# A rebuilt opening: input first, sums of squares partly on TensorE, eight input products open, weights' low parts on GpSimd

## The chip, the cores and the metric

One core of a Trainium2 chip. The time is the device time of one execution in microseconds. The engines are TensorE (PE, its weight loads PEld), VectorE (DVE), ScalarE (ACT), GpSimd (POOL) and SyncE (SP), which here issues all DMAs.

## The reference

A trunk of two layers, on x of 512 tokens by 1024 channels in float32. Each layer is a token mixer followed by a gated convolutional FFN (2816 hidden channels); both sit between norms:

```
h = rmsnorm(x, g0) * (1 + scale) + shift     # adaLN: shift, scale, gate from silu(c) @ ada_w + ada_b
x = x + gate * rmsnorm(mixer(h), g1)
```

The mixer of layer 0 is the RG-LRU: `gate_br, x_br = split(h @ w_in)`, a causal convolution of width 4 over x_br, two sigmoid gates by block-diagonal products, a first-order recurrence over the tokens, `(gelu(gate_br) * hs) @ w_out`. That of layer 1 is gated linear attention. The change is in the kernel's first sublayer, RG-LRU with the norm before it, and in helpers that all sublayers use.

## The kernel before

**Layout.** Channels lie on the 128 partitions and tokens on the free axis: x is eight tiles (KD = 8) of 128 channels by 512 tokens, in one constant buffer. A product accumulates over eight input tiles in one PSUM bank of 512 columns.

**Products in parts.** For precision each float32 operand is split into a high part (rounded to the format that PE multiplies fast, `FR`) and a low part (the rest). `mm3` issues three matmuls: high by high, high by low, low by high. For weights, `load_upto` loads a unit of up to 1024 columns into a `raw` buffer; ACT rounds it into the first half of a `w` buffer (`acopy`) and DVE subtracts to get the second half (`tt`). There are 8 `w`, 3 `raw` and 2 `araw` buffers; `mm` has 7 PSUM banks, `nr` the eighth.

**Order of the work.** Every instruction is first recorded by a wrapper of `Emit` with an engine, an estimated duration, what it reads and writes. `Sched.order` then runs a list schedule over these: SP and PE take what is ready in the order of recording, the other engines what has the longest path to the end, and a buffer is taken when its first instruction is placed. The result is a fixed order on each engine; the hardware then follows it with semaphores. So the durations in `mms`, `tt` and the others time nothing on the chip, but they do set the order.

**The opening.** In the order of recording:

1. Loads: c, x tiles 0 and 1, `par` (all column parameters, 582 columns), the identity, x tiles 2 to 7.
2. The first norm: ACT squares each tile, DVE adds the squares into one tile (`sumsq_add`), PE multiplies that by a column of ones, which gives the sums per token (`rstd_bcast`), ACT scales them, POOL takes the power -0.5 (`pow`), DVE multiplies the identity by each of four columns (a diagonal `dg`), PE multiplies a matrix of ones by that, so that the factor of each token stands on all partitions in PSUM (`rb0`).
3. c is spread over the partitions by PE (`crow`), ACT applies silu (`cact`).
4. For each input tile k: a tile `xn = x * rb0` on DVE; two adaLN columns, each of them a load of 512 KB and one DVE instruction that multiplies and sums (`ada`), finished on ACT (`ada_col`); weight unit `rgx` k; then scale and shift on ACT, rounding on ACT, the low part on DVE; then the products of this tile for NX = 6 output tiles, which stay open in six banks over all k. Tile 0 goes in two halves of 256 tokens (FH = 1).
5. Constants of the decay: some 25 instructions of 8 columns on DVE.
6. `conv4` on each of the six products: one ACT instruction and three on DVE read the bank. The other two outputs (`rgx2`) are then made one after the other, each over all k.
7. The gates: `RGG` says which gate-branch products (`gproj`, one bank, eight input tiles) come ahead of which block's gates. Blocks 0 and 3 multiply raw float32 weights, blocks 1 and 2 in parts (GFR). `recur` does the recurrence of two blocks, `gmul` the last product; `out_proj` follows, by halves of the tokens.

`rstd_from` (steps "power, diagonal, ones") serves every norm in the kernel; in the later ones it works on two columns (256 tokens) at a time, in GLA on four.

adaLN columns of the later sublayers are recorded behind the recurrence (24) and along the FFN (`ada_some`), and fill DVE where their loads have landed.

Of the kernel before, what the change touches and what calls it, by code (L numbers as in the profile page):

```python
# [15 lines left out]
P = 128  # L16
# [8 lines left out]
RGG = ((), (0,), (1,2,3,4), (5,6,7))  # L25
NX = 6
# [4 lines left out]
def unit_list():  # L31
    """Weight units in the order of their use: (key, array name, [(k, m), ...])."""
# [42 lines left out]
# column-parameter layout  # L75
PCOLS = {}
_n = 0
for _name, _w in (("norm_g", 64), ("ffn_conv_w", 2 * 3 * 44), ("ffn_conv_b", 2 * 44),
                  ("rg_conv_w", 32), ("rg_conv_b", 8), ("rg_ba", 8), ("rg_bx", 8),
                  ("rg_lambda", 8), ("gla_b_alpha", 4), ("gla_norm_g", 2), ("ada_b", 96)):  # L80
    PCOLS[_name] = (_n, _w)
    _n += _w
NPAR = _n


class Buf:
    """A tile whose place on the chip is taken when its first instruction is emitted."""
# [10 lines left out]
class View:  # L98
# [12 lines left out]
    def __getitem__(self, sl):  # L111
        """Columns of a plain view."""
        lo = sl.start or 0
        return self.buf[self.lo + lo:self.lo + (self.n if sl.stop is None else sl.stop)]
# [22 lines left out]
ENGS = ("pe", "dve", "act", "pool", "sp")  # L137


class Sched:  # L140
    """Records the kernel's instructions with their operands, orders them by a list schedule
    (deadlines from the longest path to the end, the tensor engine in program order), and
    emits them to Tile in that order."""
# [34 lines left out]
    def order(self):  # L178
# [23 lines left out]
        # allocation order per class  # L202
# [29 lines left out]
        cand = {e: [] for e in ENGS}     # (prio, idx) ready or soon ready  # L232
        wait = {e: [] for e in ENGS}     # (ready, idx)
# [11 lines left out]
        while done < n:  # L245
# [8 lines left out]
            for e in ENGS:  # L254
# [7 lines left out]
                if e == "act" and cand[e]:  # L262
                    # a change of the function table costs time: prefer the present one
                    cand[e].sort(key=lambda c: ops[c[1]].prio +
                                 (TABLE_BIAS if ops[c[1]].table not in (None, table) else 0.0))
                    for j, c in enumerate(cand[e]):
                        if can_alloc(ops[c[1]]):
                            pick = ops[c[1]]
                            del cand[e][j]
                            break  # L270
                    heapq.heapify(cand[e])
                    if pick is None:
                        continue
# [10 lines left out]
                o = pick  # L284
                for b in o.bufs:
                    if not b.live:
                        b.live = True
                        if b.cls in free:
                            free[b.cls] -= 1
                o.start = t  # L290
                dur = o.dur
                if e == "pe":
                    # the clock is halved until the engine has been busy for a while
                    if t - efree[e] > 2.5:
                        warm_at = t + 3.4
                    if t < warm_at:
                        dur *= 2
# [46 lines left out]
class Emit:  # L344
    """Instruction wrappers: costs and operands for the schedule, closures for the emission."""
# [72 lines left out]
    def mms(self, group, after=()):  # L418
        """One schedule item of consecutive matmuls: (out, lhsT, rhs, start, stop[, skip])."""
        dur = 0.0  # L420
        reads, writes = [], []
        for g in group:
            n = g[2].n
            if g[1].buf.dt == FR:
                dur += max(n, 256) * 0.4167e-3 + 0.0025
            else:
                dur += max(n, 118 if n > 1 else 100) * 1.667e-3 + 0.005
            reads += [g[1], g[2]]
            writes.append(g[0])
# [22 lines left out]
KSPLIT = 2                                  # input tiles that come one by one at a sublayer's start  # L452
NAH = 7                                     # products open at a sublayer's start
GWU = ((1, 2, 3), (0,), (0, 1))             # weights in general tiles: two FFNs' pairs, GLA's heads
FH = 1                                      # input tiles taken in halves at the start
TPE = 5                                     # output tiles whose last sum the tensor engine does
GFR = (1, 2)                                # gate blocks multiplied in parts
ADA_A, ADA_B, ADA_F = 24, 4, 4              # adaLN columns per stretch
ADAW = {2: (2, 5), 4: (0, 3, 6), 3: (1, 4, 7)}   # adaLN rows that pass through a weight slot
# [4 lines left out]
def trunk(ctx, tc, xT, wall, adaT, par_d, c_d, walpha_d, ident_d, masks_d, outT):  # L464
# [15 lines left out]
    def gtn(n):  # L480
        """A scratch view of n columns."""
        return (s.buf("gh", F32, 256) if n <= 256 else s.buf("g"))[0:n]
# [12 lines left out]
    x = [xbuf[k * S:(k + 1) * S] for k in range(KD)]  # L495
    e.load(crow[0:D].rows(1), c_d, 4096)

    for k in range(KD):
        e.load(x[k], xT[:, k, :], P * S * 4)
        if k == 1:  # L500
            e.load(par[:], par_d, P * NPAR * 4)
            e.load(ident[:], ident_d, P * P * 4)
    e.memset(ones[:], 1.0)
# [18 lines left out]
    def load_upto(i):  # L522
        while nxt[0] <= min(i, len(UNITS) - 1):
# [9 lines left out]
            if UNITS[j][0] in ingen:  # L533
                # in general tiles, which are plenty at the start of a sublayer
# [8 lines left out]
            if UNITS[j][0][0] == "gz":  # L543
                # 16 columns of either part side by side: one product serves both
# [9 lines left out]
            e.tt(w[D:D + n], raw[0:n], w[0:n].f32(), ALU.subtract)  # L554
# [34 lines left out]
    def rstd_from(nr, nt, dim, act=False):  # L589
        """nr[:, :nt]: sums per token tile -> rstd broadcast to all partitions (PSUM)."""  # L590
# [6 lines left out]
        dg = s.buf("gh", F32, 256) if nt <= 2 else gt()  # L597
        for t in range(nt):
            e.ts(dg[t * P:(t + 1) * P], ident[:], rp[t:t + 1], None, ALU.mult)
        e.mms([(nr[0:nt * P], ones[:], dg[0:nt * P], True, True)])  # L600
# [8 lines left out]
    acc0 = gt()  # L609
    for k in range(KD):  # L610
        sumsq_add(acc0[:], x[k], k == 0)
    rb0 = rstd_bcast(acc0, S, D, True)

# [1 line left out]
    cact = const(D)  # L615
    for i in range(2):
        pc = mmtile()
        e.mms([(pc[:], ones[0:P].rows(1), crow[i * S:(i + 1) * S].rows(1), True, True)])
        e.act(cact[i * S:(i + 1) * S], pc[:], AF.Silu, table="silu")

# [8 lines left out]
    def mod_cols(layer, part, k0=0, k1=KD):  # L629
        """Finish a part: 0/3 shift, 1/4 (1+scale)*norm_g, 2/5 gate*norm_g."""  # L630
# [32 lines left out]
    def h_tile(h, k, sl, rb, n, layer, part_sh):  # L663
        """h = (x * s2) * rstd + shift, in two parts."""
# [7 lines left out]
    def out_proj(src, wkey, klist, gate, nexth, yacc=None):  # L672
        """Last product of a sublayer, y = src @ W (+ yacc); x += gate * rmsnorm(y) * g; then the
        next sublayer's h, or the output. The token halves follow each other, so that the norms
        of one run beside the products of the other."""
# [4 lines left out]
        for sl in HALVES:  # L680
            acc = s.buf("gh", F32, 256)
            ys = []
            for m in range(KD):
# [9 lines left out]
                else:  # L693
                    e.tt(yv, yv, ps[0:n], ALU.add)
                    if end:
                        # the last square by itself, straight into the sum over partitions
# [15 lines left out]
            if nexth is None and sl is HALVES[1]:  # L712
                # the tensor engine, idle by now, takes part of the sums
# [35 lines left out]
    def proj_halves(keys, h_):  # L749
        """First products of a sublayer, by token halves and input tiles as these become ready."""  # L750
# [79 lines left out]
    def ada_col(part, k):  # L830
        """One column of the first norm's shift or scale."""
# [9 lines left out]
    e.stt(b1g[:], pcol("ada_b", 8, KD), 1.0, pcol("norm_g", 0, KD), ALU.add, ALU.mult)  # L841
    h = new_h()
    xps = [mmtile() for _ in range(NX)]
    for k in range(KD):
        # the normalized tile first: shift and scale come from memory later; the first tiles
        # in halves, which go faster through the engines
        parts = HALVES if k < FH else (ALL,)
        xn, hf = gt(), gt()
        hh, hl = h[k]
        for sl in parts:  # L850
            e.tt(xn[sl], x[k][sl], rb0[sl], ALU.mult)
# [3 lines left out]
        for sl in parts:  # L855
            e.act(hf[sl], xn[sl], AF.Identity, bias=mcol(0, 0, k), scale=mcol(0, 1, k))
            e.acopy(hh[sl], hf[sl])
            e.tt(hl[sl], hf[sl], hh[sl].f32(), ALU.subtract)
            for m in range(NX):
                # one reset per bank, before its first half  # L860
# [5 lines left out]
    # decay constants: softplus(-lam) = max(-lam, 0) + log1p(exp(-|lam|))  # L866
# [62 lines left out]
    def recur(ms):  # L929
# [8 lines left out]
        for m in ms:  # L938
            # th = tanh(z), a = exp(-2z): 1 - a = th (1 + a), sqrt(1 - a^2) = sqrt(th) (1 + a)
# [39 lines left out]
    def qk_evac(key, ps):  # L979
        if key[0] == "gz":  # L980
            # rows of z by the two parts of its weights; as an operand: hi, lo, hi
# [82 lines left out]
    def bcol(v, c, j):  # L1064
        """Column j of every block of c, repeated over the block."""
        return v.map(lambda a: a.rearrange("p (n c) -> p n c", c=c)[:, :, j:j + 1].to_broadcast([P, v.n // c, c]))

    def masked(atd, lv, ps, c, lo):
        """Copies the columns lo to c of every block of c where the mask of the level is set."""
# [118 lines left out]
def _unit_sources(i):  # L1188
# [3 lines left out]
    # block-diagonal gates: row tile (block, half), column tiles [wa0 wa1 wx0 wx1]  # L1192
# [58 lines left out]
```

## Time and profile before

| | us |
|---|---|
| median of 3 runs | 1185.19 (1184.75 to 1185.59) |
| span of the profiled execution, first to last instruction | 1182.5 |
| time outside that span, median less span | 2.7 |
| PE, DVE, ACT, POOL busy | 1158.9, 867.3, 553.6, 24.4 |
| first input product, dense run of them | 22.8, 23.8 |
| power -0.5 of the first norm on POOL | starts at 15.55, takes 1.56 |

The profiled execution's own time is its span with what lies around it. A share of busy time is an average over stages: the 98% of PE leaves out that PE is nearly idle in the first 24 us, and the 73% of DVE that DVE is nearly full in the first 185 us. A busy PE is also not a PE at its peak: its pace is read from the number of matmuls in a stretch.

### The profile page before, as it was taken

How to read it: one execution, taken by the hardware profiler on the slowest of the kernel's cores; microseconds unless marked ns; L12 is line 12 of the kernel's file. 1: busy time of each engine (PE TensorE's matmuls, PEld its weight loads, DVE VectorE, ACT ScalarE, POOL GpSimd, SP SyncE). 2: the span in 40 equal slices, each digit the busy share in tenths (PEclk: the TensorE clock that was granted, in tenths of full speed). 3: DMA queues.
4: the chain of work that ended last, by engine and by line, in shares of the span. 5: the costliest groups of instructions: out<-in, count | busy, mean ns of one | idle time of the engine just before them, and what ended most of it. 6: DMA issues, size and time to landing. Idle time of an engine off the chain costs nothing.

```text
span 1182.5 us, 16970 instructions
## 1 busy us (share of the span) xinstructions
PE 1158.9 (98%) x6664; PEld 1017.0 (86%) x6664; DVE 867.3 (73%) x1470; ACT 553.6 (47%) x874; POOL 24.4 (2%) x37
## 2 busy tenths in 40 slices
PE   4999999999999999999999999999999999999998
PEld 3878899988888888899999899999988888888897
DVE  7999999988988956558779767458845556645635
ACT  5688864743333324434478344254643333424421
POOL 1000001000000000000000000000000000000000
PEclk9999999999999999999999999999999999999999
DMA  8956562477787843232412211203243333332202
GB/s 338 312 170 202 200 214 73 160 249 252 249 260 223 261 126 93 88 90 59 144 55 90 72 54 55 72 27 118 72 125 97 100 91 105 90 107 90 72 1 72
DMA packets 45857, 157.44 MB, mean 133 GB/s; under 512 B 4977, under 2 KB 7281, under 8 KB 45778
## 3 DMA queue, kind: packets, MB, share of 16 engines
q1 hardware_dynamic: 45778, 156.36, 41.6%
q8 instruction: 52, 0.85, 0.3%
q14 instruction: 27, 0.22, 0.1%
HBM read 154.25 MB, written 2.10 MB: 132 GB/s over the span
## 4 chain that ended last, share of the span: by engine, by line
PE 90%; DVE 5%; ACT 3%; issue 1%; DMA 1%; SPq 0%; POOL 0%; DVEq 0%; POOLq 0%
PE mm L435 88%; ACT g L411 2%; PE nr L435 1%; DVE g L377 1%; DVE w L364 1%; ACT L411 1%; DVE g L364 1%; ACT w L416 1%; DVE gh L377 1%; DVE g L393 1%; DVE w L377 1%; DMA const<-in_xT_dram 0%; DMA raw<-in_wall_dram 0%; DVE araw L377 0%; SPq L441 0%
## 5 line engine op out<-in xcount | busy, mean ns | idle before, releaser
L435 PE MATMUL mm<-g,w 128*128 128x512 f32 (+1 forms) x5114 | 957.5, 348 | 5.6 <-ACT g L416 2.5
L435 PEld LDWEIGHTS mm<-g,w 128*128 128x128 f32 x5114 | 826.2, 189 | 130.4 <-ACT g L416 4.1
L364 DVE TENSOR_TENSOR w<-raw,w 128x1024 fp32r<-128x1024 f32 (+1 forms) x181 | 217.8, 1205 | 152.4 <-ACT w L416 152.0
L416 ACT CAST w<-raw 128x1024 fp32r<-128x1024 f32 (+1 forms) x181 | 187.2, 1036 | 206.3 <-PE mm L435 202.3
L377 DVE SCALAR_TENSOR_TENSOR g<-mm,const,g 128x511 f32<-128x511 f32 (+3 forms) x208 | 153.3, 745 | 11.2 <-ACT g L411 5.3
L364 DVE TENSOR_TENSOR g<-g,g 128x512 f32<-128x512 f32 (+4 forms) x213 | 126.2, 614 | 37.7 <-ACT g L411 19.4
L411 ACT ACTIVATE g<-mm,const 128x512 f32<-128x512 f32 (+1 forms) x148 | 102.2, 698 | 20.6 <-PE mm L435 20.5
L411 ACT ACTIVATE g<-g 128x512 f32<-128x512 f32 (+1 forms) x132 | 66.7, 540 | 96.2 <-DVE g L377 77.4
L435 PE MATMUL mm<-g,g 128*128 128x256 f32 (+4 forms) x748 | 102.1, 293 | 0.0
L435 PEld LDWEIGHTS mm<-g,g 128*128 128x128 f32 (+1 forms) x748 | 94.8, 191 | 3.8
L416 ACT CAST g<-g 128x512 fp32r<-128x512 f32 (+1 forms) x74 | 45.4, 614 | 107.7 <-DVE g L364 105.0
L377 DVE SCALAR_TENSOR_TENSOR araw<-araw,const 128x1024 f32<-128x1024 f32 x72 | 87.1, 1220 | 9.2 <-DMA araw<-in_adaT_dram 9.0
L364 DVE TENSOR_TENSOR g<-g,mm 128x512 f32<-128x512 f32 (+1 forms) x80 | 44.9, 577 | 44.5 <-PE mm L435 44.2
L364 DVE TENSOR_TENSOR gh<-gh,gh 128x256 f32<-128x256 f32 x97 | 40.4, 420 | 22.2 <-ACT gh L411 20.6
L435 PE MATMUL mm<-w,g 128*128 128x256 f32 x384 | 49.6, 288 | 0.0
L435 PEld LDWEIGHTS mm<-w,g 128*128 128x128 f32 x384 | 46.9, 192 | 1.4 <-issue 1.4
L368 POOL TENSOR_TENSOR sm<-sm,const 128x2 f32<-128x2 f32 (+1 forms) x19 | 19.4, 1022 | 1025.7 <-DVE sm L388 1018.5
L411 ACT ACTIVATE gh<-g 128x256 f32<-128x256 f32 x32 | 13.1, 416 | 51.3 <-DVE g L364 51.3
L411 ACT ACTIVATE g<-gh,const 128x256 fp32r<-128x256 f32 x48 | 21.9, 503 | 26.4 <-DVE gh L377 26.2
L411 ACT ACT_TABLE_LOAD x24 | 30.8, 1283 | 1.1 <-PEq L1242 0.7
L377 DVE SCALAR_TENSOR_TENSOR w<-w,const 128x1024 f32<-128x1024 f32 x24 | 28.8, 1217 | 0.0
L411 ACT ACTIVATE gh<-const 128x256 f32<-128x256 f32 x48 | 18.9, 414 | 20.1 <-DVE const L364 20.0
(66 smaller groups left out, 465.6 us busy)
## 6 DMA issues: line engine op xcount, KB each, us to landing
raw<-in_wall_dram SPq DMA_DIRECT2D x186, 512.0 KB, 3.7
araw<-in_adaT_dram SPq DMA_DIRECT2D x72, 512.0 KB, 4.5
w<-in_adaT_dram SPq DMA_DIRECT2D x24, 512.0 KB, 5.8
raw<-in_wall_dram SPq DMA_DIRECT2D x8, 384.0 KB, 6.7
const<-in_xT_dram SPq DMA_DIRECT2D x8, 256.0 KB, 4.1
out_dram<-const SPq DMA_DIRECT2D x8, 256.0 KB, 2.1
araw<-in_masks_dram SPq DMA_DIRECT2D x1, 512.0 KB, 5.2
const<-in_par_dram SPq DMA_DIRECT2D x1, 291.0 KB, 3.6
```

The costliest lines, as they stand in the source:

```text
L364: self.s.add(eng, dur, lambda: e.tensor_tensor(out.ap(), a.ap(), b.ap(), op=op), [a, b], [out])
L368: lambda: self.nc.gpsimd.tensor_tensor(out.ap(), a.ap(), b.ap(), op=ALU.pow), [a, b], [out])
L377: return self.nc.vector.scalar_tensor_tensor(out.ap(), a.ap(), f(sc), b.ap(), op0=op0, op1=op1, **kw)
L393: lambda: self.nc.vector.tensor_tensor_scan(out.ap(), a.ap(), b.ap(), 0.0, op0=ALU.mult, op1=ALU.add),
L411: return self.nc.scalar.activation(out.ap(), a.ap(), func, **kw)
L416: self.s.add("act", (0.095 if self._sb(a) else 0.052) + out.n * 0.8325e-3, lambda: self.nc.scalar.copy(out.ap(), a.ap()), [a], [out])
L435: r.append(self.nc.tensor.matmul(g[0].ap(), g[1].ap(), g[2].ap(), start=g[3], stop=g[4], **kw))
```

## The change

- **Loads.** c, then all eight tiles of x, then the identity. `par` is laid out anew, with norm weights and adaLN biases first, and loaded in two pieces: 160 columns behind weight unit 0, the rest (422 columns) at input tile 4. Weight unit 0 is loaded ahead of the first adaLN columns.
- **First norm.** The squares are summed in four groups (`SQ_GROUPS`): tiles 0, 1 and 7 alone, tiles 2 to 6 added by DVE as before. PE sums each group into the same four PSUM columns. The table of silu is loaded by an extra instruction at the start.
- **All norms.** No diagonal: PE multiplies the broadcast column (as the stationary operand) by the identity, one matmul per 128 tokens.
- **First tiles.** `h_tile`, as in the other sublayers: one DVE instruction for `x * scale * rstd`, one on ACT (shift and rounding), one on DVE (low part). Tile 0 reads the factor from PSUM, the others from a copy in SBUF made by ACT (`rs0`).
- **Eight products.** NX = 8: all eight outputs are open over all k; the eighth uses the `nr` bank once the factor has been read. The `rgx2` units are gone, `rgx` units have 1024 columns, and RGG is new.
- **Low parts.** The subtraction for `rgx` units 1 to 7 runs on GpSimd.
- **Scheduler.** DVE may be left empty where an instruction that is more urgent by 1.5 us becomes ready before the candidate would end (`LOOK`); durations of matmuls in `mms` are new.

Comments and docstrings are removed too. The core of the diff:

```diff
-RGG = ((), (0,), (1,2,3,4), (5,6,7))
-NX = 6
+RGG = ((0, 1), (2,), (3, 4, 5), (6, 7))
+NX = 8
...
+NPAR0 = 64 + 96
...
+LOOK = ("dve",)
...
                 o = pick
+                if e in LOOK and any(r < t + o.dur - 0.05 and ops[i].prio < o.prio - (r - t) - 1.5 and can_alloc(ops[i])
+                                     for r, i in wait[e]):
+                    heapq.heappush(cand[e], (o.prio, o.idx))
+                    continue
...
             if g[1].buf.dt == FR:
-                dur += max(n, 256) * 0.4167e-3 + 0.0025
+                dur += max(n, 256) * 0.4167e-3 + 0.0135
             else:
-                dur += max(n, 118 if n > 1 else 100) * 1.667e-3 + 0.005
+                dur += 2 * max(n * 0.8333e-3 + 0.002, 0.112)
...
+SQ_GROUPS = ((0,), (1,), (2, 3, 4, 5, 6), (7,))
...
+    e.memset(ones[:], 1.0)
     e.load(crow[0:D].rows(1), c_d, 4096)
     for k in range(KD):
         e.load(x[k], xT[:, k, :], P * S * 4)
-        if k == 1:
-            e.load(par[:], par_d, P * NPAR * 4)
-            e.load(ident[:], ident_d, P * P * 4)
-    e.memset(ones[:], 1.0)
+    e.load(ident[:], ident_d, P * P * 4)
...
             e.acopy(w[0:n], raw[0:n])
-            e.tt(w[D:D + n], raw[0:n], w[0:n].f32(), ALU.subtract)
+            e.tt(w[D:D + n], raw[0:n], w[0:n].f32(), ALU.subtract,
+                 "pool" if UNITS[j][0][0] == "rgx" and UNITS[j][0][1] > 0 else "dve")
...
         e.pow(rp[0:nt], rs[0:nt], nhalf[0:nt])
-        dg = s.buf("gh", F32, 256) if nt <= 2 else gt()
-        for t in range(nt):
-            e.ts(dg[t * P:(t + 1) * P], ident[:], rp[t:t + 1], None, ALU.mult)
-        e.mms([(nr[0:nt * P], ones[:], dg[0:nt * P], True, True)])
+        e.mms([(nr[t * P:(t + 1) * P], rp[t:t + 1].map(lambda a: a.to_broadcast([P, P]), P), ident[:], True, True)
+               for t in range(nt)])
...
-    acc0 = gt()
-    for k in range(KD):
-        sumsq_add(acc0[:], x[k], k == 0)
-    rb0 = rstd_bcast(acc0, S, D, True)
...
+    warm = const(1)
+    e.act(warm[:], ones[0:1], AF.Silu, table="silu")
...
+    nr0 = s.buf("nr")
+    sums0 = []
+    for ks in SQ_GROUPS:
+        acc0 = gt()
+        for k in ks:
+            sumsq_add(acc0[:], x[k], k == ks[0])
+        sums0.append(acc0)
+    for j, a in enumerate(sums0):
+        e.mms([(nr0[t:t + 1], a[t * P:(t + 1) * P], ones[0:1], j == 0 and t == 0, j == len(sums0) - 1, True)
+               for t in range(NT)])
+    rb0 = rstd_from(nr0, NT, D, True)
...
-    xps = [mmtile() for _ in range(NX)]
+    rs0 = gt()
+    e.acopy(rs0[:], rb0[:])
+    xps = [mmtile() if m < MMB else s.buf("nr") for m in range(NX)]
     for k in range(KD):
+        if k == 0:
+            unit("rgx", 0)
+            e.load(par[0:NPAR0], par_d[:, 0:NPAR0], P * NPAR0 * 4)
+            e.stt(b1g[:], pcol("ada_b", 8, KD), 1.0, pcol("norm_g", 0, KD), ALU.add, ALU.mult)
+        if k == 4:
+            e.load(par[NPAR0:NPAR], par_d[:, NPAR0:NPAR], P * (NPAR - NPAR0) * 4)
         parts = HALVES if k < FH else (ALL,)
-        xn, hf = gt(), gt()
-        hh, hl = h[k]
-        for sl in parts:
-            e.tt(xn[sl], x[k][sl], rb0[sl], ALU.mult)
         for part in (1, 0):
             ada_col(part, k)
         w = unit("rgx", k)
         for sl in parts:
-            e.act(hf[sl], xn[sl], AF.Identity, bias=mcol(0, 0, k), scale=mcol(0, 1, k))
-            e.acopy(hh[sl], hf[sl])
-            e.tt(hl[sl], hf[sl], hh[sl].f32(), ALU.subtract)
+            h_tile(h, k, sl, (rs0 if k else rb0)[sl], sl.stop - sl.start, 0, 0)
             for m in range(NX):
                 mm3(xps[m][sl], w, m, rr(h[k], sl), k == 0 and sl is parts[0], k == KD - 1, True)
```

More of the change, by code (lines that the diff above doesn't have):

```diff
@@ L77 @@
 _n = 0
-for _name, _w in (("norm_g", 64), ("ffn_conv_w", 2 * 3 * 44), ("ffn_conv_b", 2 * 44),
+for _name, _w in (("norm_g", 64), ("ada_b", 96), ("ffn_conv_w", 2 * 3 * 44), ("ffn_conv_b", 2 * 44),
                   ("rg_conv_w", 32), ("rg_conv_b", 8), ("rg_ba", 8), ("rg_bx", 8),
-                  ("rg_lambda", 8), ("gla_b_alpha", 4), ("gla_norm_g", 2), ("ada_b", 96)):
+                  ("rg_lambda", 8), ("gla_b_alpha", 4), ("gla_norm_g", 2)):
     PCOLS[_name] = (_n, _w)
@@ L840, in trunk @@
     b1g = const(KD)
-    e.stt(b1g[:], pcol("ada_b", 8, KD), 1.0, pcol("norm_g", 0, KD), ALU.add, ALU.mult)
     h = new_h()
-    xps = [mmtile() for _ in range(NX)]
+    rs0 = gt()
+    e.acopy(rs0[:], rb0[:])
+    xps = [mmtile() if m < MMB else s.buf("nr") for m in range(NX)]
     for k in range(KD):
+        if k == 0:
[4 more added lines that the diff above has]
+            e.load(par[NPAR0:NPAR], par_d[:, NPAR0:NPAR], P * (NPAR - NPAR0) * 4)
         parts = HALVES if k < FH else (ALL,)
-        xn, hf = gt(), gt()
-        hh, hl = h[k]
-        for sl in parts:
-            e.tt(xn[sl], x[k][sl], rb0[sl], ALU.mult)
         for part in (1, 0):
```

## The prediction

> **What bounds the kernel now.** I read the page's totals first, then the windows (stretch, its length, busy time of PE, PE's weight loads, DVE, ACT and POOL with their instructions, clock, DMA share, GB/s), then what PE waited for after 20 us (total, times, longest).
>
> ```profile
> span 1182.5 us, 16970 instructions
> PE 1158.9 (98%) x6664; PEld 1017.0 (86%) x6664; DVE 867.3 (73%) x1470; ACT 553.6 (47%) x874; POOL 24.4 (2%) x37
> ...
> L411 ACT ACTIVATE g<-mm,const 128x512 f32<-128x512 f32 (+1 forms) x148 | 102.2, 698 | 20.6 <-PE mm L435 20.5
> ...
> const<-in_par_dram SPq DMA_DIRECT2D x1, 291.0 KB, 3.6
> ...
> 10.00:20.00 10.00, 3.59 (x10) 2.28 (x10) 9.24 (x28) 3.55 (x7) 1.56 (x1) 1.00 1.03 413
> 13.00:185.00 172.00, 164.88 (x883) 138.84 (x883) 166.18 (x290) 122.91 (x198) 3.44 (x3) 1.00 0.66 225
> 24.00:58.00 34.00, 34.00 (x162) 29.07 (x163) 33.80 (x62) 21.55 (x37) 0.00 (x0) 1.00 0.90 312
> ...
> PE mm L435 <- ACT g L411: 1.1, 2, 0.7
> PE mm L435 <- DVE g L377: 0.8, 3, 0.3
> PE mm L435 <- DVE w L364: 0.8, 1, 0.8
> ```
>
> PE is the bound. Beside the first product's, PE waits some 3 us in all. So the time is when the first products start, plus PE's work (which the change keeps), plus new waits. Two things stand out. PE does almost no product before 23.8 us. And DVE is as full as PE until 185 us: 33.80 of 34 us in the input products, 166.18 of 172 us from the first adaLN column to the FFN's first tiles, 5.8 us idle. DVE is a second bound close behind.
>
> The opening itself, from the timeline (start, duration):
>
> ```profile
> 6.43 0.46 DVE L388 TENSOR_SCALAR const<-const 128x8 f32<-128x8 f32 x4
> 10.25 1.94 ACT L411 ACTIVATE g<-const 128x512 f32<-128x512 f32 x3 [0.87 <-DMA const<-in_xT_dram]
> 10.91 2.28 DVE L364 TENSOR_TENSOR g<-g,g 128x512 f32<-128x512 f32 x3 [0.21 <-ACT g L411]
> 13.19 1.22 DVE L377 SCALAR_TENSOR_TENSOR w<-w,const 128x1024 f32<-128x1024 f32 x1
> 13.25 1.87 PE L435 MATMUL nr<-const,g 128*128 128x1 f32 x8 [7.05 <-DVE g L364]
> 15.21 0.26 ACT L411 ACTIVATE sm<-nr,const 128x4 f32<-128x4 f32 x1 [0.38 <-PE nr L435]
> 15.55 1.56 POOL L368 TENSOR_TENSOR sm<-sm,const 128x4 f32<-128x4 f32 x1 [7.25 <-ACT sm L411]
> 17.27 0.86 DVE L388 TENSOR_SCALAR g<-const,sm 128x128 f32<-128x128 f32 x4
> 18.28 2.05 PE L435 MATMUL nr<-g,const 128*128 128x512 f32 x2 [3.16 <-DVE g L388]
> 21.21 1.34 DVE L364 TENSOR_TENSOR g<-const,nr 128x256 f32<-128x256 f32 x3
> 22.81 0.58 PE L435 MATMUL mm<-g,w 128*128 128x256 f32 x1 [2.48 <-ACT g L416]
> 23.81 8.46 PE L435 MATMUL mm<-g,w 128*128 128x256 f32 x47 [0.42 <-DVE g L364]
> ```
>
> It is one chain: last x tile, its square (ends 12.19), add (13.19), sums over partitions (15.12), square root (17.11), diagonal, broadcast (20.33), normalized tile, scale, cast, product.
>
> **The change, step by step.**
>
> *Loads.* par (291 KB) and the identity (64 KB) no longer lie between x's tiles: 0.36 MB at 413 GB/s is 0.9 us, at the slower start's pace up to 1.5. I take 1.1: the last square ends at 11.1 and that of x6 at 10.45. On SP's queue the adaLN tiles now follow weight unit 0 and the first 160 columns of par (0.6 MB, 1.45 us): the first lands about 0.35 us later than before, in time for the scale.
>
> *Sums.* The square of tile 7 goes straight to PE, but the group of tiles 2 to 6 is added on DVE and summed on PE ahead of it: add until 11.2, then 16 instructions at the 0.21 us of the row at 13.25, done at 14.85. That is 0.3 us earlier, not 1.1: two rounds on PE cost what the one add cost. Squares of tiles 0 and 1 are summed beside loads.
>
> *Root and broadcast.* The root stays on POOL. It waits there for DVE's adaLN instruction (see below), so it ends near 16.9. The diagonal (0.86 us, and two hand-overs) is gone; PE multiplies the broadcast column by the identity in eight 128-column instructions, a quarter of the two at 18.28 each, 2.2 us. Done at 19.2 instead of 20.33.
>
> *First tile.* Before: 2.48 us from broadcast to product, of which 0.9 is an adaLN instruction that DVE had begun. After: one DVE and one ACT instruction on 256 columns.
>
> ```profile
> 185.83 0.51 ACT L411 ACTIVATE g<-gh,const 128x256 fp32r<-128x256 f32 x1 [2.30 <-DVE gh L377]
> 1172.94 0.70 POOL L368 TENSOR_TENSOR sm<-sm,const 128x2 f32<-128x2 f32 x1 [22.33 <-DVE sm L388]
> 1173.67 0.48 DVE L388 TENSOR_SCALAR gh<-const,sm 128x128 f32<-128x128 f32 x2 [0.88 <-POOL sm L368]
> 1174.94 0.48 DVE L377 SCALAR_TENSOR_TENSOR gh<-g,const,nr 128x256 f32<-128x256 f32 x1 [0.79 <-PE nr L435]
> ```
>
> 0.48 and 0.51 with hand-overs make 1.2; the look-ahead on DVE (it leaves the engine empty for an urgent instruction) should keep most of the 0.9 away, but the order is fixed ahead of time, so I leave 0.2 of it. First product near 20.6, the dense run (after the low part) near 21.4 instead of 23.81: **2.4 us gained**. Bounds: 0.9 (all waits return) to 3.5.
>
> *Eight products.* 192 products of 512 columns either way; only their order changes. Each input tile now holds PE for 24 x 0.228 = 5.5 us instead of 4.1:
>
> ```profile
> L435 PE MATMUL mm<-g,w 128*128 128x512 f32 x134 | 30.5, 389 | 0.0
> ...
> L377 DVE SCALAR_TENSOR_TENSOR w<-w,const 128x1024 f32<-128x1024 f32 x24 | 28.8, 1217 | 0.0
> L364 DVE TENSOR_TENSOR w<-raw,w 128x1024 fp32r<-128x1024 f32 x22 | 26.7, 1219 | 0.4 <-ACT w L416 0.3
> L364 DVE TENSOR_TENSOR g<-g,g 128x512 fp32r<-128x512 f32 x19 | 12.5, 684 | 0.8 <-ACT g L416 0.8
> L364 DVE TENSOR_TENSOR w<-raw,w 128x768 fp32r<-128x768 f32 x8 | 7.6, 949 | 0.0
> L377 DVE SCALAR_TENSOR_TENSOR g<-mm,const,g 128x511 f32<-128x511 f32 x8 | 5.8, 741 | 0.0
> L364 DVE TENSOR_TENSOR g<-const,nr 128x512 f32<-128x512 f32 x7 | 4.7, 677 | 0.0
> L388 DVE TENSOR_SCALAR g<-const,sm 128x128 f32<-128x128 f32 x4 | 0.9, 278 | 0.0
> ```
>
> (PE from 30 to 60 us, 30.5/134 = 0.228; DVE from 13 to 185 us; last number the mean in ns.) Afterwards all eight banks are taken. The first is free after the convolution of product 0: one ACT instruction (0.7) and three of DVE (0.74), with the hand-overs about 3.2 us, while PE still has seven products' last parts, 7 x 0.68 = 4.8 us. No wait, if DVE takes it up within 1.6 us; else the excess is lost once.
>
> *DVE's budget, 13 to 185 us.* Gone: eight low parts of 768 columns (7.6), two units of 1024 for the products that came later (2.4), diagonals (0.9 for the first norm, and two pairs of 0.48 like the row at 1173.67 for the later ones). Added: unit 0 at 1024 columns (1.2) and the decay constants that ran before 13 us, like the row at 6.43 (about 1.5; they now wait for par's second part). The h tiles stay two instructions of 0.68. Net -9.2.
>
> *Low parts of units 1 to 7 on GpSimd.* No row shows such an instruction. POOL's nearest row is a memset:
>
> ```profile
> L448 POOL MEMSET g<- x9: 99/520/529, 573.9 to 711.4; 128x512 f32 x5, 128x1 f32 x4
> ```
>
> 0.52 us for 512 columns written; 1024 columns with two reads lie between 1.04 and three such passes, 3.1. I take two passes, 2.1. The units land every 3.8 us (1.5 MB at 413 GB/s) and PE needs one in 5.5, so POOL itself hides it. What it may cost DVE is the open price: 0 to 7 x 2.1 = 14.7 us. I take a third, because a tile's 2 x 1.22 + 2 x 0.68 = 3.8 us leave DVE 1.7 us in 5.5: +5. DVE then still ends 4 us lighter, enough for a PE that runs 2.4 us ahead.
>
> *Other norms.* Every root loses its diagonal. At the end, from root to first use is 1.3 us; four 128-column instructions in place of 0.48 on DVE make about 0.85: **0.45**. At sublayer starts the 1.9 us of waits for L411 and L377 tiles can lose up to 0.48 per norm; DVE's queue decides most of it: **0.6**. The look-ahead and the new product costs reorder all of DVE's work; I put zero, -1 to +1.
>
> **Sum:** 2.4 + 0.45 + 0.6 = 3.45. The profiled span is 1182.5, 2.7 below the median of 1185.19; I take the rest as fixed. 1185.2 - 3.5 = **1181.7 us**.
>
> **Rivals.**
>
> *A. GpSimd locks DVE out (slower).* Rows for one direction are there:
>
> ```profile
> 204.33 1.21 DVE L364 TENSOR_TENSOR w<-raw,w 128x1024 fp32r<-128x1024 f32 x1
> 204.49 1.61 POOL L368 TENSOR_TENSOR sm<-sm,const 128x2 f32<-128x2 f32 x1 [11.87 <-DVE sm L388]
> ...
> 573.86 0.78 POOL L448 MEMSET g<- 128x512 f32 x5
> 573.94 0.59 DVE L388 TENSOR_SCALAR gh<-const,sm 128x128 f32<-128x128 f32 x2 [0.59 <-POOL sm L368]
> ```
>
> The same root takes 0.70 with DVE idle and 1.61 here, ending 0.56 after DVE's instruction. DVE in turn takes 0.59 beside a memset where it takes 0.48 alone. If DVE stands still for all of each low part, the budget is -9.2 + 14.7 = +5.5, as much as the 5.8 us of idle, which are waits for other engines and will not all fill. DVE ends its work at 185 us 2 to 5.5 us late, PE with it; less 0.6 for the end: 1186.6 to 1190. It decides from about 1.3 us lost to each low part, where DVE's budget stands as before. [...] Against: a tile's loop leaves DVE 1.7 us. Chance 0.26. [...]
>
> *B. PE is warm early (faster).* In the opening PE steps 0.213 us per sum (1.87 for 8), at the end half of it:
>
> ```profile
> 1171.99 0.61 PE L435 MATMUL nr<-const,gh 128*128 128x1 f32 x4 [0.62 <-ACT gh L411]
> ```
>
> After, PE has work from 2.4 us on with the early sums. If it keeps the fast step, the last 16 sums save 1.7, the broadcast 1.1, the first dozen products 1.1: up to 3.9 more, 1177.8; with half of it 1179.8. Against: gaps of some 2 us remain, and before 23.8 it never was fast. Chance 0.14. [...]
>
> *C. The gain is eaten.* PE starts 2.4 us earlier but meets DVE and ACT, which follow each other through the recurrence, where they stood; or the convolution of product 0 comes late. Then only 0.45 and some tenths stay: 1183.5 to 1186. For it: DVE's 166.18 of 172. Chance 0.20.
>
> **How the numbers follow.** My case 0.40, A 0.26, B 0.14, C 0.20. 0.2% (2.4 us) is about what a measurement tells from no change. My case spans 1180 to 1183, a tenth of it inside that; so faster 0.51, same 0.23, slower 0.26. Range 1178 to 1189: it leaves out the fast half of B and the end of A.
>
> **What would show it.** First product of the dense run at 21 to 22 us; sums done near 14.9; no diagonals on DVE; low parts on POOL near 2.1 us; products of 512 columns still at 0.228 us and no PE wait above 1 us up to 185 us. Wrong if low parts take 3 us or more, if DVE's adaLN instructions show well over 1.22 us, or if PE waits at the out-projection (near 148 us) or at the FFN's start (near 183 us) for DVE by several us.

## The result, and the profile after

The changed kernel takes **1215.76 us** (1214.08 to 1216.27), the kernel before 1184.97 beside it: ratio 1.0256 (1.0242 to 1.0271), slower by 30.8 us, where 1181.7 had been forecast. The profiled execution's span is 1214.1 us, 31.6 above the 1182.5 of before.

The page's totals:

```profile
span 1214.1 us, 17088 instructions
PE 1178.8 (97%) x6752; PEld 1038.0 (85%) x6752; DVE 869.1 (72%) x1410; ACT 549.2 (45%) x865; POOL 43.9 (4%) x44
```

GpSimd's largest group (line, engine, operation, tile, shapes, count, busy us, mean ns, idle before):

```profile
L371 POOL TENSOR_TENSOR w<-raw,w 128x1024 fp32r<-128x1024 f32 x7 | 18.1, 2591 | 25.9 <-ACT w L423 25.9
```

PE still looks 97% busy. The windows (columns as in the prediction) show where it is not:

```profile
13.00:185.00 172.00, 152.32 (x721) 125.14 (x721) 154.94 (x233) 101.82 (x155) 21.26 (x9) 0.95 0.58 203
24.00:58.00 34.00, 24.63 (x112) 20.23 (x111) 31.60 (x55) 10.10 (x17) 17.21 (x7) 0.90 0.65 227
```

What PE waited for after 24 us (total, times, longest) shows for whom:

```profile
PE mm L442 <- ACT g L418: 8.0, 1, 8.0
PE mm L442 <- DVE g L384: 3.9, 2, 2.1
PE mm L442 <- ACT g L423: 3.6, 1, 3.6
PE nr L442 <- POOL sm L375: 2.6, 4, 0.7
PE nr L442 <- DVE gh L371: 1.8, 6, 0.3
PE mm L442 <- DVE g L1092: 1.5, 1, 1.5
```

Before, PE ran all of the stretch from 24 to 58 us; now it runs 24.63 of 34, and the clock column, 1.00 before, says 0.90. The waits in this list are 21.4 us; before they were 3.1. The clock is the second price. It fell to half in four stretches:

```profile
40.20:47.00 6.80, 3.69 (x8) 2.62 (x9) 6.80 (x10) 2.64 (x5) 2.24 (x1) 0.50 0.70 247
67.50:70.90 3.40, 3.40 (x10) 2.63 (x9) 3.40 (x6) 2.19 (x4) 0.00 (x0) 0.50 0.51 190
166.50:173.30 6.80, 6.53 (x29) 6.24 (x30) 6.55 (x10) 2.81 (x8) 0.00 (x0) 0.50 0.42 137
658.00:668.20 10.20, 9.74 (x45) 9.74 (x46) 7.37 (x16) 5.39 (x13) 0.00 (x0) 0.50 0.00 0
```

PE worked 23.4 us in them; by the granted clock of 0.50 that is the work of 11.7 us at 1.00. Each begins in a wait or at most 1.1 us after one: 8.0 us (35 to 43), 1.9 (64), 3.6 (163) and 1.5 (657). The last is the plainest, at the 56 products of 64 columns that open a GLA stretch. The timeline of before:

```profile
631.46 6.36 PE L435 MATMUL mm<-g 128*128 128x64 f32 x56
```

and of after:

```profile
654.21 2.79 PE L442 MATMUL mm<-g 128*128 128x64 f32 x24
658.46 7.09 PE L442 MATMUL mm<-g 128*128 128x64 f32 x32 [1.46 <-DVE g L1092]
```

A wait of 1.46 us in the middle, and the other 32 start 0.213 us apart instead of 0.112: 3.2 us more. With that, the wait cost some three times its length.

So the 31.6 us, from the start times of PE's instructions: the first product comes 1.4 earlier (-1.4), but the slow start (products of 256 columns 0.213 us apart, 0.119 later), which ends at 26.5 us (26.7 before), covers more products (+0.8); waits behind it +18.3; the four stretches at a clock of 0.50 +11.7. That makes 29.4. The other 2.1 lie in the spacing of PE's instructions themselves and are not traced further; e10 below, without one new instruction, has 3.1 of the same kind.

**The opening came nearly as forecast**, PE in the timeline:

```profile
11.79 3.57 PE L442 MATMUL nr<-const,g 128*128 128x1 f32 x16 [2.28 <-DVE g L371]
17.53 2.08 PE L442 MATMUL nr<-const,sm 128*128 128x128 f32 x8 [2.17 <-POOL sm L375]
21.40 2.81 PE L442 MATMUL mm<-g,w 128*128 128x256 f32 x10 [1.79 <-ACT g L418]
```

The dense run starts at 21.9 instead of 23.81. Of these 1.9 us some 1 us is left once the slow start is over: at 29 us PE has started 43 products of 256 columns, 34 before, and one takes 0.119 us. All of it was lost by 43 us. GpSimd, DVE, PE and ACT around it:

```profile
24.44 2.38 POOL L371 TENSOR_TENSOR w<-raw,w 128x1024 fp32r<-128x1024 f32 x1 [6.97 <-ACT w L423]
31.21 4.73 POOL L371 TENSOR_TENSOR w<-raw,w 128x1024 fp32r<-128x1024 f32 x2
...
24.47 2.90 DVE L384 SCALAR_TENSOR_TENSOR g<-const,const,g 128x512 f32<-128x512 f32 x1
29.74 0.74 DVE L384 SCALAR_TENSOR_TENSOR g<-const,const,g 128x512 f32<-128x512 f32 x1
31.28 2.34 DVE L395 TENSOR_SCALAR const<-const 128x8 f32<-128x8 f32 x1 [0.80 <-POOL const L375]
33.89 2.07 DVE L371 TENSOR_TENSOR const<-const,const 128x8 f32<-128x8 f32 x1
...
34.46 0.84 PE L442 MATMUL nr<-g,w 128*128 128x512 f32 x3
43.31 2.01 PE L442 MATMUL mm<-g,w 128*128 128x512 f32 x3 [8.01 <-ACT g L418]
...
42.20 0.29 ACT L418 ACTIVATE const<-const,const 128x1 f32<-128x1 f32 x1 [11.85 <-DVE w L384]
```

The same DVE instruction takes 0.74 alone and 2.90 beside a low part on GpSimd, and ends 0.55 us after it. Eight columns take 2.34 and 2.07 instead of 0.17, and end with it. These are the decay constants: now that par's second part lands late (21.7 us), their chain stands in DVE's order from 29.1 to 39.9 us, ahead of the adaLN columns of the third input tile. ACT waits 11.85 us for those columns, PE 8.01 for ACT. Over all seven low parts seven DVE instructions are stretched in this way, by 1.6 to 2.2 us each, 14 us in all.

### The profile page after: what moved, and what is told of

It reads as the page before. It is cut to its first block, busy times and chain, and to the rows that moved or that the text cites. A ratio compares the mean times of both kernels' runs of the same rounds, so it can differ in the third digit from the quotient of the medians.

```text
span 1214.1 us, 17088 instructions
## 1 busy us (share of the span) xinstructions
PE 1178.8 (97%) x6752; PEld 1038.0 (85%) x6752; DVE 869.1 (72%) x1410; ACT 549.2 (45%) x865; POOL 43.9 (4%) x44
## 4 chain that ended last, share of the span: by engine, by line
PE 81%; DVE 9%; ACT 6%; issue 2%; POOL 1%; DMA 0%; SPq 0%; DVEq 0%; POOLq 0%; ACTq 0%
PE mm L442 79%; ACT g L418 3%; DVE g L384 2%; PE nr L442 2%; DVE gh L371 2%; ACT L418 1%; DVE const L371 1%; DVE w L384 1%; DVE g L371 1%; ACT w L423 1%; POOL sm L375 1%; DVE g L400 1%; DVE gh L384 0%; DVE araw L384 0%; DMA const<-in_xT_dram 0%
## 5 line engine op out<-in xcount | busy, mean ns | idle before, releaser
L442 PE MATMUL mm<-g,w 128*128 128x512 f32 (+1 forms) x5093 | 958.9, 350 | 17.5 <-ACT g L418 9.8
L423 ACT CAST w<-raw 128x1024 fp32r<-128x1024 f32 x179 | 186.7, 1045 | 215.3 <-PE mm L442 204.7
L371 DVE TENSOR_TENSOR w<-raw,w 128x1024 fp32r<-128x1024 f32 x172 | 208.6, 1216 | 81.2 <-ACT w L423 80.3
L384 DVE SCALAR_TENSOR_TENSOR g<-mm,const,g 128x510 f32<-128x510 f32 (+3 forms) x205 | 152.4, 747 | 96.0 <-ACT g L418 89.4
L371 DVE TENSOR_TENSOR g<-g,g 128x512 f32<-128x512 f32 (+3 forms) x201 | 119.3, 614 | 31.6 <-ACT g L418 21.3
L423 ACT CAST g<-g 128x512 fp32r<-128x512 f32 (+1 forms) x65 | 40.3, 621 | 114.4 <-DVE g L371 111.2
L418 ACT ACT_TABLE_LOAD x24 | 30.8, 1283 | 1.2 <-PEq L1259 0.7
L442 PEld LDWEIGHTS mm<-g 128*128 128x128 f32 x224 | 29.0, 212 | 1.9 <-DVE g L1092 1.6
L442 PE MATMUL mm<-g 128*128 128x64 f32 x224 | 29.0, 295 | 1.5 <-DVE g L1092 1.5
```

Source lines behind the costliest of these rows:

```text
L371: self.s.add(eng, dur, lambda: e.tensor_tensor(out.ap(), a.ap(), b.ap(), op=op), [a, b], [out])
L384: return self.nc.vector.scalar_tensor_tensor(out.ap(), a.ap(), f(sc), b.ap(), op0=op0, op1=op1, **kw)
L418: return self.nc.scalar.activation(out.ap(), a.ap(), func, **kw)
L423: self.s.add("act", (0.095 if self._sb(a) else 0.052) + out.n * 0.8325e-3, lambda: self.nc.scalar.copy(out.ap(), a.ap()), [a], [out])
L442: r.append(self.nc.tensor.matmul(g[0].ap(), g[1].ap(), g[2].ap(), start=g[3], stop=g[4], **kw))
```

## The experiments

All ratios are to the kernel before, on the same chip; intervals of single kernels are some 0.0015 to either side.

**e1: the low parts back on DVE.** `-  "pool" if ... else "dve")  +  ALU.subtract)`

> The changed kernel with one edit: the low parts of units 1 to 7 go back to VectorE. [...] Order theory (the decay constants, moved behind the second part of par, stand ahead of tile 2's shift column on VectorE): the chain takes about 5.5 us without locks instead of 10.7, so a wait of 2 to 4 us stays; 1198 to 1206 us. [...]

1208.35 us, 1.0199 (1.0182 to 1.0216), slower than the order theory's 1198 to 1206, and than the 1183 to 1190 of the lock theory, by which it is the low parts on GpSimd that hold DVE up. The 8 us wait is gone, and 7.3 us of 30.8. Most of the loss at the end is elsewhere: PE waits at 148, 193, 209 and 648 us, and the granted clock is 0.95 over 152 to 185 us and 0.97 over 185 to 250, both 1.00 before. Along the way the low parts cost more: PE's sums for the first norm behind the out-projection start 24.0 us later than before in the changed kernel and 8.4 us later in e1; between there and the end the changed kernel loses 8 us more and e1 16.

**e2: par's second part directly behind the first.** `-  if k == 4:  +  if k == 0:`

> The changed kernel with one edit: the second part of par is loaded right behind the first, so that the decay constants can run on VectorE before the first tiles. Order theory: the 8.0 us wait and its half-clock stretch go, 9 to 12 us less, 1204 to 1207 us. Lock theory: the seven low parts cost VectorE the same 16 us, only at other places; 1210 to 1216 us.

1216.79, 1.0269 (1.0253 to 1.0284): outside the order theory, 0.8 us above the lock theory. The late constants alone are not it: a wait of 6.8 us at 34 stays.

**e3: the kernel before with the low parts of units 1 to 7 on GpSimd** (e1's line the other way).

> The kernel before with one edit: the low parts of units 1 to 7 (768 columns, about 1.8 us each on GpSimd) run on GpSimd. Lock theory: VectorE loses 7 x (1.8 - 0.9) = 6.5 us net in a stage where it has 5.8 us idle, and the order knows nothing of it; PE waits of several us come in the input products, 1189 to 1197 us. If GpSimd works beside VectorE: 6 us less for VectorE, 1183 to 1185 us.

1197.1, 1.0104 (1.0089 to 1.0119): +12.2 us, 11.1 of it there by the norm at 168 us. The order is planned anew here too, so the 12.2 us are a DVE held up and a new order together. The timeline shows which of DVE's instructions take longer under the low parts:

```profile
25.69 3.73 POOL L364 TENSOR_TENSOR w<-raw,w 128x768 fp32r<-128x768 f32 x2 [2.71 <-ACT w L416]
...
25.86 2.47 DVE L364 TENSOR_TENSOR g<-const,nr 128x512 f32<-128x512 f32 x4
28.26 2.25 DVE L377 SCALAR_TENSOR_TENSOR w<-w,const 128x1024 f32<-128x1024 f32 x1
```

Four normalized tiles, which read the norm from PSUM (nr), run through at 0.62 us each under the low parts; the adaLN instruction, with both tiles in SBUF, takes 2.25 instead of 1.22. With one tile in the row, the changed kernel shows both: the 2.34 us are a `TENSOR_SCALAR`, which takes 0.17 alone, while the `RECIPROCAL` of eight columns behind it ran under the next low part in its usual 0.20. The change had copied the norm to SBUF for tiles 1 to 7, and the instruction that reads the copy took 2.90 instead of 0.74 (above).

**e4: e1 and e2 together.**

> Both edits of the last two on the changed kernel. If lock and order are the whole loss of the first 70 us, no PE wait above 0.5 us stays between 22 and 75 us, and the gain of 2.4 us at the start is kept there; 1181 to 1187 us, the upper end if the waits at the out-projection and in GLA stay. If the opening is late for another reason (eight products, the way the banks come free): a wait stays near the end of the input products, 1190 us or more.

1203.97, 1.0163 (1.0147 to 1.0178). First product at 20.77, no wait above 0.3 us until 146 us: an opening without fault, and still 19 us lost at the end. The low parts and the late part of par are thus shown to make the waits of the first 70 us; with these gone the expectation had 1181 to 1187. Of the next four, three undo one part each on e4, and the last undoes all three.

**e5: no look-ahead** (`LOOK = ()`). **e6: the planner's old matmul durations.** **e7: diagonals back.** **e8: all three undone.**

> The kernel of e4 (low parts on VectorE, par early; 1204.0 us) without the look-ahead on VectorE. If leaving VectorE empty makes the loss of e4 (about 14 us of PE waits after 140 us, and half-clock stretches behind 151, 209 and 646 us): 1186 to 1192 us. If the durations of the matmuls or the norms make it: within 3 us of 1204.

> The kernel of e4 with the planner's former matmul durations. Nothing on the chip differs but the order of instructions. If the new durations (each fast matmul 11 ns longer) put norm sums and copies at worse places: the waits of PE for the sums' tiles (2.5 us near 205 us, six of 0.2 to 0.4) and for GLA's masks (1.5 us near 644 us, half clock behind it) go; 1188 to 1194 us. Else within 3 us of 1204.

> The kernel of e4 with the diagonal back in all norms. If PE's waits for the root on GpSimd (0.7, 0.7, 0.9, 0.7, 0.4, 0.2 us in e4) come from PE standing at the broadcast by itself, they go, 3 to 5 us less, and the first product starts 1 us later: 1200 to 1202 us. If a VectorE step takes their place: 1204 to 1206 us.

> The kernel of e4 with all three undone: no look-ahead, former durations, diagonals. What is left is the opening: x first, four groups of squares, h tiles in three instructions, eight products, the new order of the gates. If eight products and the order of the gates are good or neutral: 1181 to 1185 us. If they cost by themselves (the wait of 3.4 us before the out-projection with its half-clock stretch): 1188 to 1192 us.

1210.88 (1.0222), 1199.32 (1.012), 1210.48 (1.0217), 1192.32 (1.006, 1.0045 to 1.0075). The first three fall where neither of their theories said. Taking out look-ahead or the new norm makes it worse, the old durations make it 5 us better, all three out make it best: the parts don't add. What they share is that each changes the order, so the next ones, from e10 on, put single parts on the kernel before.

**e9: e8 with six open products** (`NX = 6`, the old RGG).

> The kernel of e8 (1192.3 us) with six open products and the former order of the gates; of the change only the loads, the four groups of squares, the three-instruction tiles and the early silu table are left. If eight products and the new order of the gates make the 7 us that e8 lost: 1183 to 1187 us, and the waits of 1.4 and 1.3 us near 142 and 151 us go. If the early part does (the first product came at 23.2 us in e8 and the next at 24.9): 1190 to 1193 us.

1192.21, 1.0059 (1.0044 to 1.0074). Eight products and the gates' order make no difference here. The 7 us are in what is left of the change, and since that was planned anew too, they can't be parted from its order.

**e10: the kernel before, the planner's durations alone.** Only the order differs, by:

```
-                dur += max(n, 256) * 0.4167e-3 + 0.0025
+                dur += max(n, 256) * 0.4167e-3 + 0.0135
...
-                dur += max(n, 118 if n > 1 else 100) * 1.667e-3 + 0.005
+                dur += 2 * max(n * 0.8333e-3 + 0.002, 0.112)
```

> The kernel before with the planner's new matmul durations alone. If they are wrong for the order as such: 1188 to 1192 us, with waits of PE at norms and a half-clock stretch in GLA near 650 us. If they hurt only in a VectorE that is late already: 1184 to 1187 us.

**1213.26, 1.0237** (1.0222 to 1.0252): +28 us without one new instruction, far above both theories. Its timeline, DVE and PE at the output products:

```profile
151.38 3.70 DVE L377 SCALAR_TENSOR_TENSOR g<-g,g 128x512 f32<-128x512 f32 x6
155.00 2.33 DVE L393 TENSOR_TENSOR_SCAN g<-g,g 128x512 f32<-128x512 f32 x2
158.43 1.22 DVE L364 TENSOR_TENSOR w<-raw,w 128x1024 fp32r<-128x1024 f32 x1
159.71 2.51 PE L435 MATMUL mm<-g,w 128*128 128x256 f32 x10 [8.26 <-DVE w L364]
```

The same scans and the same low part in the timeline of before:

```profile
146.42 2.33 DVE L393 TENSOR_TENSOR_SCAN g<-g,g 128x512 f32<-128x512 f32 x2
...
149.85 1.22 DVE L364 TENSOR_TENSOR w<-raw,w 128x1024 fp32r<-128x1024 f32 x1
```

The recurrence's last gates and scans stand ahead of the weight's low part, as they did before, but run 8.6 us later. DVE was not overloaded: it did 87.43 us of work from 58 to 152 where it did 92.39 before, and waited 4.5 us for adaLN loads, which arrive later in the new order. A lower clock follows: 0.90 over 152 to 185 us, 0.99 over 200 to 520 and 0.94 over 640 to 700, all 1.00 before.

The last of these stretches ties the durations to the changed kernel. From the norm at 571.5 us to GLA's at 647.6 (times of before) eight kernels lose 6.1 to 8.5 us, the changed kernel 7.9: after, e1, e2, e4, e5, e7, e10 and e13, which are just those that plan with the fast matmuls' new duration. At the 64-column products there PE waits for DVE: 1.5 us in after, e1 and e4, 1.7 in e13, 2.3 in e10. Behind it the clock is 0.50 for 10.2 us in after; in e10 the 0.94 over 640 to 700 us comes to some 7 us at 0.50. The other eleven lose at most 1.5 us in that stretch, whatever else they share with the change.

**e11: the kernel before without diagonals. e12: with look-ahead alone.**

> The kernel before with the norms without diagonals alone. By the prediction: first product 1 us earlier, end 0.45 us shorter, 1183 to 1184 us. If PE now stands at the root on GpSimd: 1186 to 1190 us.

> The kernel before with VectorE's look-ahead alone. If it helps as it did in e4 (7 us less than without): 1180 to 1184 us. If VectorE has no time to stand empty: 1187 to 1192 us.

e11: 1186.38, 1.0012 (1.0003 to 1.0022). e12: 1199.41, 1.0121 (1.0104 to 1.0137), 7 us above the worse of its theories. Look-ahead does what it says, the first product comes 1 us earlier; at the first FFN ACT and PE then wait for adaLN columns that DVE left for later:

```profile
191.85 0.51 ACT L417 ACTIVATE g<-gh,const 128x256 fp32r<-128x256 f32 x1 [5.04 <-DVE const L370]
...
192.41 0.58 PE L441 MATMUL mm<-g,w 128*128 128x256 f32 x1 [6.38 <-ACT g L417]
```

**e13 to e16: is it a lead that DVE lost, or is any other order worse?** All are the kernel before with other planned durations: the fast matmuls' new one alone, the fp32 one's alone, the fast one 5% shorter (`0.95 * (...)`), and half of its step (`+ 0.0080`).

> The kernel before with the planner's new duration for the fast (two-part) matmuls alone: 0.0135 us instead of 0.0025 us on top of 0.4167 ns per column, so 0.2268 us planned for 512 columns where 0.2158 us stood; the fp32 matmuls keep their old planned duration. Only the order of the instructions differs. Theory L (lead): a planned TensorE that is a few per cent too quick makes DVE's due times early, and with true durations the lead is gone: nearly all of the +28 us of both durations together, 1208 to 1215. Theory R (rough): every change of the planner's numbers falls upon some other order, and its price has no direction: anywhere from 1185 to 1215.

> The kernel before with the planner's new duration for the fp32 matmuls alone (0.857 us for 512 columns where 0.858 stood, 0.224 us for one column where 0.172 stood). Theory L: some tens of sums per norm are planned later by 0.05 us each, and TensorE's bulk as before: within 3 us of the kernel before, 1183 to 1188. Theory R: a new order with a price of its own, 1190 to 1215.

> The kernel before with the planned duration of the fast matmuls cut by 5% (0.205 us for 512 columns, where 0.2158 stood and a trace shows 0.228). Theory L: DVE gets more lead still, so no new wait of TensorE: 1180 to 1187. Theory R: as far off as the same step in the other direction, 1195 to 1215.

> The kernel before with 0.0080 us in place of 0.0025 on top of each fast matmul in the planner, half of the change's step. Theory L: about half of the price, 1195 to 1203. Theory R: no relation to the whole step: either near 1186 or 1205 and above.

1209.02 (1.0206), 1190.83 (1.0048), 1195.23 (1.0088), 1190.86 (1.0058); no interval reaches down to 1.003. Longer durations cost +5.8 and then +24: the direction of theory L (lead), though e16 lies under L's 1195 to 1203 and fits R's "near 1186 or 1205 and above" no better. The shorter one costs +10.2 and the fp32 one +5.8, where L said nothing: theory R (rough). Neither alone holds. The order of before is better than its neighbours on both sides, and the worst one comes from the durations that are nearest the measured 0.228 us for 512 columns.

**e17, e18: the instructions without the new order.** e17 plans with the diagonals and issues nothing for them; e18 also moves par and the identity behind x.

```
         for t in range(nt):
             e.ts(dg[t * P:(t + 1) * P], ident[:], rp[t:t + 1], None, ALU.mult)
+            s.ops[-1].fn = lambda: []
```

> The kernel before without the diagonals of all norms, the instructions of e11, but not planned again: the planner still sees the diagonals, its order is kept for every engine, and a diagonal then issues nothing (the broadcast goes by 128-column products with the identity). Theory O (the order is the price): the first tile comes 0.8 us earlier, the end 0.45, the sublayers' starts some 0.3: 1183 to 1184.2, below e11's 1186.4. Theory C (an earlier TensorE meets the vector engine where it stood): 1184.7 to 1185.5.

> e17 and x first, again with the planned order of the kernel before: par and the identity are loaded behind x's last tile, eight columns of par (for the decay constants, which so stay in the opening) in a load of their own at par's old place, and four short vector instructions that read par stand behind the last sum of squares. Theory O: x's last tile lands about 1 us earlier and all that follows it: 1182 to 1183.3, the first of these kernels that beats both. Theory C: no more than e17, 1184.5 to 1185.5.

**1184.18, 0.999** (0.9981 to 0.9999), and 1184.39, 0.9993 (0.9984 to 1.0001). Where e11 lost 1.1 us to the kernel before, the same instructions in the old order win 1.0: planning anew cost some 2. e17 is the best time of all, though within 0.2% of before; it lies at the edge of theory O, e18 between its two. In the profile the opening's gain doesn't last. The dense run begins 0.98 us earlier, but its slow products last until 28.1 us, not 26.7, and at 28.1 us PE has done no more than before (15 of them in this row, 0.213 us apart):

```profile
22.83 3.57 PE L435 MATMUL mm<-g,w 128*128 128x256 f32 x15 [0.42 <-DVE g L364]
...
184.90 0.60 PE L603 MATMUL nr<-const,sm 128*128 128x128 f32 x4
185.26 0.96 PE L435 MATMUL mm<-g,w 128*128 128x256 f32 x6
```

The last two rows are a broadcast and what follows it; the same place before:

```profile
184.68 0.59 PE L435 MATMUL nr<-gh,const 128*128 128x256 f32 x2
184.92 1.06 PE L435 MATMUL mm<-g,w 128*128 128x256 f32 x6
```

A broadcast of four small products holds PE for 0.36 us, one of two large products for 0.24. From start to start over the whole trace that is 10.45 us against 7.72. But it is no loss: the six products behind it take 0.96 us instead of 1.06, so that from the broadcast to their end it is 1.32 us against 1.30, and all of PE's work from the first product on, the slow start reckoned at the later pace, comes to 1148.9 us in e17 and 1149.1 before. e18 gained nothing by the earlier x. Its last tile lands at 10.48 instead of 11.53, but DVE comes to the last three adds no sooner: the adds ahead of them end 0.27 us later than before, and three short constants follow these:

```profile
10.37 0.17 DVE L395 TENSOR_SCALAR const<-const 128x8 f32<-128x8 f32 x1
...
10.89 2.28 DVE L371 TENSOR_TENSOR g<-g,g 128x512 f32<-128x512 f32 x3
```

## Why the prediction was wrong, step by step

- *Loads, sums, root, broadcast, first tile*: right to within a microsecond. Sums done at 15.4 (14.85 said), root 17.5 (16.9), broadcast 19.6 (19.2), first product 21.4 (20.6), dense 21.9 (21.4). But the 2.4 us of the sum counted the earlier start in full; 1.9 came, and some 1 us of that was left after the slow start.
- *"The look-ahead and the new product costs reorder all of DVE's work; I put zero, -1 to +1."* **This step failed**: alone on the kernel before, the durations cost +28 us (e10) and the look-ahead +14 (e12). Within the change, 7.9 us at GLA go with the durations, and undoing durations, look-ahead and norms together on e4 takes off 12.0. No row of before could price a new order at zero: DVE's 166.18 of 172 us said that nothing may be late.
- *Low parts on GpSimd*: **the second step that failed.** Each takes 2.59 us (2.1 said), and seven of DVE's instructions took 1.6 to 2.2 us longer beside one: "a third" (+5) was 14 us of DVE's time, nearly the 14.7 that the prediction gave as the most. In time, e3 prices it at +12.2 with a new order, e1 at 7.3 within the change. Rival A was right that DVE is held up; its 1190 lies 7 us under e3, of which the clock explains 1.7 (0.95 over 24 to 58 us, which is 3.4 us at 0.50) and the rest is open.
- *DVE's budget, decay constants "about 1.5"*: they hold DVE's order for over 10 us, with a power on GpSimd (1.64 us) among them and two of them stretched under low parts (2.34 and 2.07 instead of 0.17). Before, most of them filled gaps of the opening; moved behind par they fill the tightest stretch.
- *Broadcast and other norms*: of the 0.45 at the end 0.36 came (the 10.11 us from the last sum of the last norm to the end became 9.75 in the changed kernel and 9.76 in e11); in e17 only 0.01, as its order keeps eight other products ahead of the broadcast there. The 0.6 at sublayer starts shows in no run.
- *Eight products*: right, no price seen (e9 against e8).
- *Rivals B and C*: PE wasn't fast early (0.213 us per product until 26.5 us). C's forecast, a gain that doesn't last, came in e17 and e18, at 1184.2 to 1184.4, but not shown is its mechanism, engines met where they stood: in e17 it was the slow start, to 28.1 us, that took the gain.
- Of the signs named as "wrong if" two came: a wait at the out-projection (3.6 us at 163, for ACT) and an adaLN instruction well over 1.22 us (one took 3.43). At the FFN's start no wait was above 0.3 us. They were given too small a chance.

Left open: why half of the durations' step costs 5.8 us and the whole 24, and whether true durations with another rule for due times would plan a better order. The single parts (28, 14, 12, 7, 0, 1 us) sum to twice the 30.8 of all together. Undone one after the other, low parts and par give 11.7 of it, durations, look-ahead and norms 12.0, the rest of the opening 7.1; another sequence would give other shares, as e5 to e8 show, so beyond the stretch at GLA no share is a part's own.

## What to carry to other kernels

An order that is planned ahead is part of the kernel: when an edit touches the planner's numbers, run the edit with the old order and the order without the edit, and only then speak of either. On a kernel where a second engine is 97% full behind the bound, price each new wait of the bound engine with the slower clock that may follow it (here 1.46 us brought 3.2 more), and each small instruction moved there from an idle stretch at its place in the queue, not at its duration. Before work goes to GpSimd, look at which DVE instructions will run beside it: here those that read two tiles from SBUF took 2.07 to 3.43 us in the changed kernel instead of 0.17 to 1.22, those that read the norm from PSUM kept their 0.62 in e3, and of two that read one tile one was held up (2.34) and one was not (0.20).

## What the hardware showed

From 26.5 us on, the granted clock in the trace of after changes between 1.00 and 0.50. The stretches between its changes are 13.653, 6.827, 20.480, 3.413, 95.573, 6.827, 484.69 and 10.240 us, the first at 1.00 and every second one at 0.50. The slow products of the start end 2.9 us after the dense run's start before and 5.3 in e17, which hides a gain of 1 us in the opening.

The length of a wait alone doesn't decide whether a lower clock follows: behind 1.46 us (after, at 657) the clock was 0.50 for 10.2 us, behind 1.88 us (after, at 64) for 3.4, and e3, which waits 1.6 us at 51, shows 0.95 over 24 to 58 us; but behind 2.05 us (after, at 56) it was 1.00 until 67.5, and behind 2.30 us (e14, at 151) 1.00 over 152 to 185. What tells these waits apart was not shown. So one wait cost nothing more here, and another 3.2 us more.
